# A transformer block on one core: the byte offsets of TensorE's two operands, two more column pairs by block products, four additions moved

## The chip, the cores and the metric

The kernel runs on one core of a Trainium2 chip. A core has five engines with queues of their own: TensorE (PE in the profile; its weight loads are listed as PEld), VectorE (DVE), ScalarE (ACT), GpSimd (POOL) and SyncE (SP, which here issues nearly all DMAs). The metric is the device time of one execution in microseconds (us). For the kernel before it is 1021.69 us, the median of three runs (1021.38 to 1025.06).

## The reference

One decoder block on x of 512 tokens by 1024 features, all in float32. Three sub-layers, each behind an RMSNorm whose result is scaled and shifted by vectors computed from c; a final RMSNorm ends it.

```python
u = modulate(rmsnorm(h, g_norm_ffn1[l]), sh1, sc1)
h = h + 0.5 * gt1 * swiglu(u, w_ffn1_in[l], w_ffn1_out[l])
u = modulate(rmsnorm(h, g_norm_mix[l]), sh2, sc2)
h = h + gt2 * token_mixing(u, cos, sin, w_in[l], ...)
u = modulate(rmsnorm(h, g_norm_ffn2[l]), sh3, sc3)
h = h + 0.5 * gt3 * swiglu(u, w_ffn2_in[l], w_ffn2_out[l])
...
def swiglu(u, w_in, w_out):
    a, b = jnp.split(u @ w_in, 2, axis=-1)
    return (jax.nn.silu(a) * b) @ w_out
```

The hidden width of `swiglu` is 2816, that is 22 tiles of 128. The token mixer is one wide projection of u, a pooling branch, dilated attention in three groups, two gates and an output projection. The change touches the two `swiglu` layers (FFN 1 and FFN 2 below) and where operands lie in memory; it does not change what is computed.

## The kernel before

Everything is kept transposed: features on the 128 partitions, tokens along the free dimension. h is eight tiles `H` of 128 x 512.

**Split operands.** TensorE runs its matmuls on float32r operands. For accuracy each operand is split into a rounded part and the rest: weights into `whi` and `wlo`, u into `UH` and `UL`, the hidden activations into `HI` and `HK`. A product is three matmuls, hi x hi, hi x lo and lo x hi (`mm3`, lines 321 to 325; `product`, lines 703 to 712, for the block products). In both the weights are the stationary operand, 128 x 128, and u or the hidden tile is the moving operand, of 512 or 256 columns.

**The weight stream.** Weights come in chunks of 128 x 1024 (some narrower), in the order of `self.order`, which `plan` (line 144) writes down for the whole kernel. A chunk is loaded to one of three `raw` buffers on SP's queue (`fetch`), rounded by ScalarE into the ring `whi` (`split_hi`, line 280) and the rest is written by VectorE into the ring `wlo` (`split_lo`, line 292). The rings hold `RING` columns; `room` (line 235) finds the place of the next chunk. `look` runs the split a few chunks ahead of the one that TensorE takes. In the built program `whi` starts at byte 13440 and `wlo` at byte 42112 of each partition, both 128 modulo 256, and every 128 x 128 tile of weights starts at that offset, since 128 columns are 512 bytes.

**Pairs and block products.** The input side of a FFN is worked in pairs j = 0 to 21: tile j of a and tile j of b. A plain pair (`ffn_pair`, line 653) is 2 x 8 x 3 = 48 matmuls of 512 columns. Two pairs together can be done by `duo` (line 714), which multiplies 2 x 2 blocks (features halved, tokens halved) with seven block products in place of eight, 7 x 24 = 168 matmuls of 256 columns. This asks for sums and differences of u's blocks (`u_steps`, line 664: four additions, then four splits into `S` tiles, named SH and SL in the profile) and for differences of weight chunks (`make`, line 222, on VectorE). u's four blocks lie in the tile `X`; two of these blocks, once added up, give the place for the weight differences (`self.X`), the two others become two more raw buffers. `PLAIN` says below which j pairs are plain: 8 in FFN 1, 4 in FFN 2.

**Order of FFN 1.** The row-by-row stage (`startup`, line 1385) goes through the eight tiles of u as they are normalised and fills all eight PSUM banks with the products of pairs 0 to 3 (lines 1481 to 1486, 192 matmuls of 512 columns). `ffn` (line 815) then works in the five `PARTS`: it computes pairs until two beyond those that the part needs, then the output stage of the part: eight output tiles of 128 x 512 over the part's hidden tiles. So part 0 has pairs 4 and 5 and its output stage, part 1 pairs 6 and 7, the block product of pairs 8 and 9, and its output stage, and so on. The output stages pop one entry of `self.todo` for each output tile; in part 0 these are the additions and splits of `u_steps`, in parts 2 and 3 the steps of the angles for the rotary embedding (`trig`). The last part ends in `out_tail` (line 482) with matmuls of 256 columns, whose first half of tokens feeds the next norm while the second half runs; `head` (line 600) of the next stage begins with matmuls of 256 columns for the same reason.

**Beside it.** The modulation vectors are computed by VectorE, one row of 128 x 1024 after another (`ada_do`, line 346, 1.2 us each, with a load of 512 KB on SP's queue). `bg` runs one. Rows 16 to 23 go beside pairs 4 and 5; rows 24 to 47 beside the tiles of pairs 6 and 7 (four) and the output stages of parts 1, 2 and 3 (eight, eight and four). FFN 2 has no such rows.

**Where u lies.** `UH` and `UL` are placed by `place_u` (line 455) at 0, 16 or 0 columns of a buffer that starts at 64 modulo 256 bytes, so at 64 for FFN 1 and FFN 2 and at 128 for the mixer. The hidden tiles, the mixer's tiles and `S0` start at 128, `S1` and `S2` at 64, after a filler `padb` of 48 columns (line 811).

Of the kernel before, what the change touches and what calls it, by code (L numbers as in the profile page):

```python
# [8 lines left out]
F32 = mybir.dt.float32  # L9
F32R = mybir.dt.float32r  # L10
# [100 lines left out]


FIRST = 4
RING = 7 * 1024


U_AT = (0, 16, 0)

PLAIN = {0: 8, 2: 4}
PARTS = ((0, 4), (4, 8), (8, 12), (12, 16), (16, 22))  # L120
NH = 6

# [14 lines left out]
class Kernel:  # L137
# [6 lines left out]
    def plan(self):  # L144
        (i1, o1), mix, (i2, o2) = chunk_widths()
        self.chunks = []
        for name, ws in (("wf1i", i1), ("wf1o", o1), ("wmix", mix), ("wf2i", i2), ("wf2o", o2)):
            off, rec = 0, []
            for w in ws:
                rec.append((name, off, w))  # L150
                off += P * w
            self.chunks.append(rec)
        f1i, f1o, mx, f2i, f2o = self.chunks


        self.loads, self.order, self.last = [], [], {}

        def plain(recs):
            for r in recs:
                n = len(self.loads)  # L160
                self.loads.append(r)
                self.last[n] = len(self.order)
                self.order.append((r[2], n, ("raw", n), None))

        def blocks(recs):
            n = len(self.loads)
            self.loads.extend(recs)
            r11, r12, r22, r21 = (("raw", n + i) for i in range(4))
            x0, x1 = ("x", 0), ("x", 1)
            for need, src, make in ((0, r11, None), (1, x0, (x0, r12, r11)), (2, x1, (x1, r22, x0)), (3, r21, None),  # L170
                                    (3, r12, (r12, r22, r12)), (3, r22, None), (3, x0, (x0, r21, x1))):
                for j, x in enumerate((r11, r12, r22, r21)):
                    if x == src or (make and x in make):
                        self.last[n + j] = len(self.order)
                self.order.append((D, n + need, src, make))

        def ffn(n, ins, outs, first):
            j, at = first, 0
            if first:
                plain(ins[:KT])  # L180
                at = KT
            for part, (k0, k1) in enumerate(PARTS):
                while j < pairs_before(n, part):
                    if j < PLAIN[n]:
                        plain(ins[at:at + 2])
                        j, at = j + 1, at + 2
                    else:
                        blocks(ins[at:at + 4])
                        j, at = j + 2, at + 4
                plain(outs[part * KT // 2:(part + 1) * KT // 2] if part + 1 < len(PARTS) else outs[-KT:])  # L190

        ffn(0, f1i, f1o, FIRST)
        base = len(self.order)
        plain(mx)
        ffn(2, f2i, f2o, 0)
        self.fetched = self.done = self.made = 0
        self.pos, self.held, self.retired, self.half = 0, None, [], None
# [37 lines left out]
    def room(self, i, held):  # L235


        w, u, at, pieces = self.order[i][0], self.unit(i), self.top, []
        for c in range(0, w, u):
            if at % RING + u > RING:  # L240
                at += RING - at % RING
            o = at % RING
            if pieces and pieces[-1][0] + pieces[-1][1].stop - pieces[-1][1].start == o:
                pieces[-1] = (pieces[-1][0], slice(pieces[-1][1].start, c + u))
            else:
                pieces.append((o, slice(c, c + u)))
# [10 lines left out]
    def split_hi(self):  # L257
# [2 lines left out]
        i = self.done  # L260
        if self.half or i == len(self.order):
            return False
        got = self.room(i, held)
        if got is None:
            assert i >= self.pos, "no room"
# [12 lines left out]
                    parts.append((slice(o + x.start - c.start, o + x.stop - c.start), x))  # L278
        for y, x in parts:
            self.nc.scalar.activation(self.hi[:, y], r[:, x], AF.Copy)  # L280
        if i + 1 < len(self.order) and self.order[i + 1][3] and self.order[i + 1][1] < self.fetched:
            self.make(i + 1)
        self.half = (r, parts)
        return True
# [170 lines left out]
    def place_u(self, n):  # L455
        self.UHv, self.ULv = (x[:, U_AT[n]:U_AT[n] + KT * T] for x in (self.UHall, self.ULall))
        self.UH, self.UL = ([x[:, k * T:(k + 1) * T] for k in range(KT)] for x in (self.UHv, self.ULv))

    def norm_steps(self, n, hs):

        t, done = {}, [0]
# [20 lines left out]
    def out_tail(self, ms, ksrc, gate, nxt, squares):  # L482
# [7 lines left out]
        for h, hs in enumerate((A, Bh)):  # L490
            for m in ms:
# [10 lines left out]
                for i, (hi, lo, uh, ul) in enumerate(ks):  # L502
                    if h == 1 and m == ms[1] and i == 3:
                        self.stats_t(self.B[6], A)
                    if h == 1 and m == ms[2] and i == 1:
                        self.spread(self.B[6], A)
                        self.place_u(nxt)
# [156 lines left out]
    def u_steps(self, n):  # L664
# [18 lines left out]
        def whole(u, k):  # L683
# [1 line left out]
            hi, lo = (y.rearrange("p (k t) -> p k t", k=KT)[:, x, :HT] for y in (self.UHv, self.ULv))  # L685
            return lambda: v.tensor_tensor(u.rearrange("p (k t) -> p k t", k=4), hi, lo, op=OP.add)

        last = split(3, a12)
        return ([whole(a11, 0), whole(a12, 4)] if n else []) + [add(a22, a21, a22, OP.add), split(0, a22), add(a21, a11, a21, OP.subtract), split(2, a21),
                add(a11, a22, a11, OP.subtract), split(1, a11), add(a12, a12, a11, OP.subtract)], last  # L690

    def step(self):

# [84 lines left out]
    def ffn2(self):  # L778
        self.put, self.now = [], 0
        bk = [self.nb() for _ in range(4)]  # L780
        self.head(2, bk, AF.Silu)
        self.todo, last = self.u_steps(2)
# [116 lines left out]
    def beside_out(self, part):  # L899

        if part == 0:
# [433 lines left out]
    def build(self):  # L1335
# [12 lines left out]
        self.UHall = tl("UH", KT * T + 16, F32R)  # L1348
        cst, self.eps = tl("cst", 163), tl("eps", 1)
        self.ULall = tl("UL", KT * T + 16, F32R)  # L1350
        self.place_u(0)
# [33 lines left out]
    def startup(self):  # L1385
# [166 lines left out]
```

## Time and profile before

| what | value |
|---|---|
| median of three runs | 1021.69 us (1021.38 to 1025.06) |
| the profiled execution, its own time | 1025.08 us |
| its span in the profile | 1023.3 us |
| granted TensorE clock | 0.998 of full speed |
| row-by-row stage of FFN 1 | 19.8 to 64.7 us |
| rest of FFN 1, with the tail | 64.7 to 366.4 us |
| mixer, from its head to its tail | 366.4 to 671.8 us |
| FFN 2, from its head | 671.8 to 1023.3 us |
| split of a 128 x 1024 chunk: ACT, then DVE | 1.05 us, 1.22 us |
| bytes from memory, mean rate | 135.8 MB, 135 GB/s |

The profile is one execution taken by the hardware profiler. An engine's busy time counts its instructions; the matmuls are pipelined, so the duration of one matmul in the timeline (0.28 us for 256 columns, 0.39 for 512) overlaps the next, and the price of a matmul is the distance from its start to the next one's. A stretch filled with equal matmuls and without waits gives this price as its length divided by their number. The three runs and the profiled execution differ by 3.7 us in all.

### The profile page before, as it was taken

Reading aid. Unit: us, or ns where it says so; the run is one execution under the profiler, and the core shown is the slowest. Engines: PE = TensorE matmul, PEld = TensorE weight load, DVE = VectorE, ACT = ScalarE, POOL = GpSimd, SP = SyncE. Lnnn points to the kernel's source line nnn. Section 1 sums busy time; section 2 is a strip of 40 time slices with the busy share of each in tenths; the row PEclk is TensorE's granted clock in tenths of the full one; section 3 lists DMA queues with packets and bytes.
Section 4 is the critical chain, followed back from the end, with each engine's and each line's share of the span. In section 5 each row is a group of like instructions: output and inputs, shape, how many; then the busy total and the mean of one; then the engine's idle time right before and its main releaser. Section 6 shows DMA issues by size and latency. Waiting matters only on the chain.

```text
span 1023.3 us, 15508 instructions
## 1 busy us (share of the span) xinstructions
PE 1012.1 (99%) x6364; PEld 914.9 (89%) x6364; DVE 753.2 (74%) x1082; ACT 434.8 (42%) x638; POOL 26.0 (3%) x30
## 2 busy tenths in 40 slices
PE   8999999999999999999999999999999999999997
PEld 7888898989999899889988888998899899998997
DVE  6969879889786777779446776577787776676754
ACT  5453352534445552334314333454365354352552
POOL 0000000000000000006100000000000000000001
PEclk9999999999999999999999999999999999999999
DMA  8856365555533513222154774322244234241312
GB/s 315 285 177 256 112 238 162 172 162 188 165 115 106 157 35 103 62 83 83 32 185 156 268 263 127 104 63 72 94 155 135 83 103 145 84 144 45 112 32 83
DMA packets 43113, 139.60 MB, mean 136 GB/s; under 512 B 4897, under 2 KB 8225, under 8 KB 43042
## 3 DMA queue, kind: packets, MB, share of 16 engines
q1 hardware_dynamic: 42354, 137.95, 41.3%
q8 instruction: 50, 0.82, 0.3%
q10 hardware_dynamic: 688, 0.66, 0.2%
q14 instruction: 21, 0.17, 0.1%
HBM read 135.82 MB, written 2.77 MB: 135 GB/s over the span
## 4 chain that ended last, share of the span: by engine, by line
PE 95%; DVE 3%; DMA 1%; ACT 0%; issue 0%; DVEq 0%; ACTq 0%
PE bank L323 17%; PE bank L324 17%; PE bank L325 17%; PE bank L710 10%; PE bank L712 10%; PE bank L711 10%; PE bank L1486 1%; PE bank L1484 1%; PE bank L1482 1%; PE bank L1080 1%; PE bank L1259 1%; PE bank L1411 1%; PE bank L1260 1%; PE bank L1261 1%; PE bank L1028 1%; PE bank L1057 1%
## 5 line engine op out<-in xcount | busy, mean ns | idle before, releaser
L292 DVE TENSOR_TENSOR wlo<-raw,whi 128x1024 fp32r<-128x1024 f32 (+2 forms) x151 | 175.5, 1165 | 69.0 <-ACT whi L280 68.8
L280 ACT ACTIVATE whi<-raw 128x1024 fp32r<-128x1024 f32 (+2 forms) x151 | 150.4, 1003 | 42.6 <-DVE raw L228 39.8
L323 PE MATMUL bank<-UH,whi 128*128 128x512 f32 (+1 forms) x432 | 159.0, 368 | 0.0
L324 PE MATMUL bank<-UL,whi 128*128 128x512 f32 (+1 forms) x432 | 154.9, 359 | 0.2 <-DVE UL L452 0.2
L325 PE MATMUL bank<-UH,wlo 128*128 128x512 f32 (+1 forms) x432 | 154.9, 359 | 0.0
L323 PE MATMUL bank<-HI,whi 128*128 128x512 f32 (+1 forms) x406 | 146.8, 362 | 0.0
L324 PE MATMUL bank<-HK,whi 128*128 128x512 f32 (+1 forms) x406 | 146.5, 361 | 0.0
L325 PE MATMUL bank<-HI,wlo 128*128 128x512 f32 (+1 forms) x406 | 146.5, 361 | 0.0
L710 PE MATMUL bank<-UH,whi 128*128 128x256 f32 x512 | 141.6, 277 | 0.0
L711 PE MATMUL bank<-UL,whi 128*128 128x256 f32 x512 | 141.6, 277 | 0.0
L712 PE MATMUL bank<-UH,wlo 128*128 128x256 f32 x512 | 141.6, 277 | 0.0
L292 DVE TENSOR_TENSOR wlo<-X,whi 128x1024 fp32r<-128x1024 f32 (+2 forms) x88 | 104.4, 1188 | 39.5 <-ACT whi L280 39.3
L710 PE MATMUL bank<-SH,whi 128*128 128x256 f32 x384 | 107.1, 279 | 0.3 <-ACT u L717 0.3
L711 PE MATMUL bank<-SL,whi 128*128 128x256 f32 x384 | 106.9, 278 | 0.0
L712 PE MATMUL bank<-SH,wlo 128*128 128x256 f32 x384 | 106.9, 278 | 0.0
L280 ACT ACTIVATE whi<-X 128x1024 fp32r<-128x1024 f32 (+2 forms) x88 | 89.3, 1028 | 33.1 <-DVE X L228 32.1
L711 PEld LDWEIGHTS bank<-UL,whi 128*128 128x128 f32 x512 | 96.1, 188 | 0.3
L710 PEld LDWEIGHTS bank<-UH,whi 128*128 128x128 f32 x512 | 96.1, 188 | 0.3
L712 PEld LDWEIGHTS bank<-UH,wlo 128*128 128x128 f32 x512 | 96.4, 188 | 0.0
L325 PEld LDWEIGHTS bank<-UH,wlo 128*128 128x128 f32 x432 | 81.3, 188 | 12.8
L324 PEld LDWEIGHTS bank<-UL,whi 128*128 128x128 f32 x432 | 81.5, 189 | 12.3 <-issue 0.5
L323 PEld LDWEIGHTS bank<-UH,whi 128*128 128x128 f32 x432 | 81.4, 189 | 11.9 <-issue 0.5
(225 smaller groups left out, 1748.5 us busy)
## 6 DMA issues: line engine op xcount, KB each, us to landing
ada<-wada SPq DMA_DIRECT2D x47, 512.0 KB, 5.0
raw<-wmix SPq DMA_DIRECT2D x44, 512.0 KB, 3.9
raw<-wf1i SPq DMA_DIRECT2D x34, 512.0 KB, 4.5
raw<-wf2i SPq DMA_DIRECT2D x30, 512.0 KB, 3.6
X<-wf2i SPq DMA_DIRECT2D x14, 512.0 KB, 3.5
cs<-wada SPq DMA_DIRECT2D x12, 512.0 KB, 3.5
AR<-wada SPq DMA_DIRECT2D x12, 512.0 KB, 3.9
raw<-wf2o SPq DMA_DIRECT2D x12, 512.0 KB, 3.6
```

The costliest lines, as they stand in the source:

```text
L280: self.nc.scalar.activation(self.hi[:, y], r[:, x], AF.Copy)
L292: self.nc.vector.tensor_tensor(self.lo[:, y], r[:, x], self.hi[:, y], op=OP.subtract)
L323: M(ps, hi, uh, start=start, stop=False)
L324: M(ps, hi, ul, start=False, stop=False)
L325: M(ps, lo, uh, start=False, stop=stop)
L710: M(o, hi, uh, start=start and p == 0 and k == 0, stop=False, skip_group_check=True)
L711: M(o, hi, ul, start=False, stop=False, skip_group_check=True)
L712: M(o, lo, uh, start=False, stop=k == 3, skip_group_check=True)
L1028: M(S[:, o + i * P:o + i * P + P], qz[:, (2 * i + h) * P:(2 * i + h + 1) * P], k[:, toks], start=True, stop=True)
L1057: nc.tensor.transpose(b[:, i * P:i * P + P], p[:, i * P:i * P + P], self.ident)
L1080: M(o, pt[:, blk * P:blk * P + P], v, start=i == 0, stop=i == len(srcs) - 1)
L1259: M(b, self.UH[k][:, c::4], hi, start=k == 0, stop=False)
```

## The change

Four parts.

- u is placed at 128 modulo 256 bytes for all three sub-layers, by fillers of 16 columns; `place_u` goes. A chunk in the set `shifted` starts 16 columns (64 bytes, `SHIFT`) further in the ring, at 192 modulo 256 bytes. Shifted are all block products' chunks, the first four chunks of the mixer and of FFN 2 (their heads), the last three of FFN 1, the last two of the mixer and the last four of FFN 2 (their tails). The ring has 128 columns more. `S0` moves to 192, `S1` and `S2` to 128.
- `PLAIN[0]` goes from 8 to 6: pairs 6 and 7 of FFN 1 are done by a block product.
- `u_steps` returns additions and splits apart. For FFN 1 the four additions run at the end of the row-by-row stage, ahead of the silu of pairs 0 to 3; the splits are popped in part 0's output stage. FFN 2 runs them in the same order as before.
- A flag `ready` keeps weight differences from being made until these splits are issued, since they are written over u's blocks.

```diff
-RING = 7 * 1024
-U_AT = (0, 16, 0)
-PLAIN = {0: 8, 2: 4}
+RING = 7 * 1024 + 128
+SHIFT = 16
+PLAIN = {0: 6, 2: 4}
...
         def blocks(recs):
             n = len(self.loads)
+            self.shifted.update(range(len(self.order), len(self.order) + 7))
...
+        def shift(i):
+            self.shifted.update(range(len(self.order) - i, len(self.order)))
...
                     if j < PLAIN[n]:
                         plain(ins[at:at + 2])
+                        if n and j < 2:
+                            shift(2)
...
         ffn(0, f1i, f1o, FIRST)
+        shift(3)
         base = len(self.order)
         plain(mx)
+        self.shifted.update(range(base, base + 4))
+        shift(2)
         ffn(2, f2i, f2o, 0)
+        shift(4)
...
     def room(self, i, held):
+        shift = SHIFT if i in self.shifted else 0
+        at += (shift - at) % 64
         for c in range(0, w, u):
             if at % RING + u > RING:
-                at += RING - at % RING
+                at += RING - at % RING + shift
...
     def split_hi(self):
+        if self.order[i][3] and not self.ready:
+            return False
...
     def u_steps(self, n):
-        last = split(3, a12)
-        return ([whole(a11, 0), whole(a12, 4)] if n else []) + [add(a22, a21, a22, OP.add), split(0, a22), add(a21, a11, a21, OP.subtract), split(2, a21),
-                add(a11, a22, a11, OP.subtract), split(1, a11), add(a12, a12, a11, OP.subtract)], last
+        adds = [add(a22, a21, a22, OP.add), add(a21, a11, a21, OP.subtract), add(a11, a22, a11, OP.subtract),
+                add(a12, a12, a11, OP.subtract)]
+        return ([whole(a11, 0), whole(a12, 4)] if n else []) + adds, [split(2, a21), split(1, a11), split(0, a22), split(3, a12)]
...
     def open_sums(self):
         for i in range(3):
+            if i < 2:
+                bp.tile([P, (SHIFT, 64 - SHIFT)[i]], F32, name=f"padb{i}")
             self.S.append([bp.tile([P, 4 * HT], F32R, name=f"S{x}{i}") for x in "HL"])
-            if i == 0:
-                bp.tile([P, 48], F32, name="padb")
...
     def beside_out(self, part):
-            self.todo, last = self.u_steps(0)
+            self.todo, last = self.splits[:3], self.splits[3]
+            self.ready = False
+            self.todo.append(lambda: setattr(self, "ready", True))
...
     def startup(self):
         self.bg_fetch()
+        adds, self.splits = self.u_steps(0)
+        for f in adds:
+            f()
         for j in range(FIRST):
```

More of the change, by code (lines that the diff above doesn't have):

```diff
@@ L156, in plan @@
         self.loads, self.order, self.last = [], [], {}
+        self.shifted = set()
         def plain(recs):
@@ L192, in plan @@
         ffn(0, f1i, f1o, FIRST)
+        shift(3)
         base = len(self.order)
         plain(mx)
+        self.shifted.update(range(base, base + 4))
+        shift(2)
         ffn(2, f2i, f2o, 0)
+        shift(4)
         self.fetched = self.done = self.made = 0
+        self.ready = True
         self.pos, self.held, self.retired, self.half = 0, None, [], None
@@ L280, in split_hi @@
             self.nc.scalar.activation(self.hi[:, y], r[:, x], AF.Copy)
-        if i + 1 < len(self.order) and self.order[i + 1][3] and self.order[i + 1][1] < self.fetched:
+        if i + 1 < len(self.order) and self.order[i + 1][3] and self.ready and self.order[i + 1][1] < self.fetched:
             self.make(i + 1)
@@ L453, in norm_b @@
                                             op0=OP.add, op1=OP.subtract)
-    def place_u(self, n):
-        self.UHv, self.ULv = (x[:, U_AT[n]:U_AT[n] + KT * T] for x in (self.UHall, self.ULall))
-        self.UH, self.UL = ([x[:, k * T:(k + 1) * T] for k in range(KT)] for x in (self.UHv, self.ULv))
     def norm_steps(self, n, hs):
@@ L506, in out_tail @@
                         self.spread(self.B[6], A)
-                        self.place_u(nxt)
                         step = self.norm_steps(nxt, A)
@@ L781, in ffn2 @@
         self.head(2, bk, AF.Silu)
-        self.todo, last = self.u_steps(2)
+        adds, (s2, s1, s0, last) = self.u_steps(2)
+        self.todo = adds[:3] + [s0, adds[3], s2, adds[4], s1, adds[5]]
         do = lambda n: [self.todo.pop(0)() for _ in range(n)]
@@ L1347, in build @@
         self.H = [tl(f"H{k}", T) for k in range(KT)]
-        self.UHall = tl("UH", KT * T + 16, F32R)
+        tl("pad0", 16)
+        self.UHv = tl("UH", KT * T, F32R)
         cst, self.eps = tl("cst", 163), tl("eps", 1)
-        self.ULall = tl("UL", KT * T + 16, F32R)
-        self.place_u(0)
+        tl("pad1", 16)
+        self.ULv = tl("UL", KT * T, F32R)
+        self.UH, self.UL = ([x[:, k * T:(k + 1) * T] for k in range(KT)] for x in (self.UHv, self.ULv))
         self.AR = tl("AR", 2 * T)
```

## The prediction

> **What bounds the kernel now.** I read three views: the page for the busiest engine and the chain, the busy times by stretch for the price of each stage, and the timeline of one stretch for the spacing of matmuls. "PE" is TensorE, "DVE" VectorE, "ACT" ScalarE.
>
> ```profile
> PE 1012.1 (99%) x6364; PEld 914.9 (89%) x6364; DVE 753.2 (74%) x1082; ACT 434.8 (42%) x638; POOL 26.0 (3%) x30
> PE 95%; DVE 3%; DMA 1%; ACT 0%; issue 0%; DVEq 0%; ACTq 0%
> ```
>
> The span is a stream of matmuls, and 95% of the chain that ended last is PE. A busy PE can still hide waits, so the stretches are next. Columns: stretch, its length, then busy time and instructions of PE, weight loads, DVE, ACT and GpSimd, then clock and DMA.
>
> ```profile
> 64.70:87.10 22.40, 22.40 (x98) 18.05 (x97) 18.00 (x25) 11.19 (x16) 0.00 (x0) 1.00 0.59 208
> 87.10:108.90 21.80, 21.80 (x98) 18.04 (x97) 19.85 (x26) 6.77 (x8) 0.00 (x0) 1.00 0.52 181
> 108.90:131.30 22.40, 22.40 (x98) 17.95 (x97) 16.93 (x21) 6.46 (x8) 0.00 (x0) 1.00 0.45 137
> 131.30:150.50 19.20, 19.20 (x170) 19.20 (x169) 15.72 (x16) 12.19 (x15) 0.00 (x0) 1.00 0.66 232
> ...
> 373.00:390.30 17.30, 17.30 (x147) 17.30 (x146) 11.10 (x21) 6.82 (x11) 0.00 (x0) 1.00 0.30 92
> 678.80:695.20 16.40, 16.40 (x147) 16.40 (x146) 10.40 (x20) 10.53 (x21) 0.00 (x0) 1.00 0.24 70
> ```
>
> In order: FFN 1's pairs 4 and 5, its first output stage, pairs 6 and 7 (each 96 matmuls of 512 columns; the counts include neighbours cut by the border), the block products of pairs 8 and 9 (168 of 256 columns), and 144 matmuls of 256 columns of the mixer's head and of FFN 2's head. The clock is 1.00 in all. Equal work differs: 22.40 against 21.80 us is 233.3 against 227.1 ns for one matmul of 512; 17.30 against 16.40 is 120.1 against 113.9 ns for one of 256. What differs is where the moving operand starts. The weights (whi, wlo) start at 128 modulo 256 bytes throughout. u of FFN 1 and 2 starts at 64, all other moving operands, u of the mixer too, at 128. Call an operand in step with the weights when both start at the same place modulo 128, out of step when they are 64 apart. So: 512 columns, in step 227, out of step 233; 256 columns, in step 120, out of step 114. The timeline has the second pair inside one block product, starts in the first column:
>
> ```profile
> 131.27 0.28 PE L710 MATMUL bank<-UH,whi 128*128 128x256 f32 x1
> ...
> 134.00 0.28 PE L710 MATMUL bank<-SH,whi 128*128 128x256 f32 x1
> ...
> 136.86 0.29 PE L710 MATMUL bank<-SH,whi 128*128 128x256 f32 x1
> ```
>
> 24 matmuls on u (64) take 2.73 us, 113.8 ns each; the next 24, on S0 (which starts at 128), 2.86 us, 119.2 ns. Nothing waits in either.
>
> **The change part by part.** After it u starts at 128 everywhere. Weights start at 192 (SHIFT) in all work of 256 columns, except the tails' first tile (m = 4 of FFN 1, m = 3 of FFN 2, m = 5 of the mixer) and the rows of v, and stay at 128 for 512 columns. S0 moves to 192, S1 and S2 to 128.
>
> 1. Row-by-row stage, 192 matmuls of 512 columns, 19.8 to 64.7 us: out of step to in step. 44.9 x 21.80/22.40 = 43.7: -1.2 us. DVE sets each row's inputs every 5.32 us (line 452's starts 46.07 and 51.39), PE then needs 5.45 a row, so PE stays the bound.
> 2. Pairs 4, 5, and FFN 2's pairs 2, 3 (22.40 us from 695.2): -0.6 each, -1.2 us.
> 3. Pairs 6 and 7 become one block product: 22.4 less 19.2: -3.2 us.
> 4. The 16 block products that stay, and FFN 2's head: out of step before and after, S0 in step before and after: 0, if the difference of the two starts is what counts. No row has weights at 192, so the bounds are 114 and 120 ns; I take 114, the row with the same difference.
> 5. Tails and the mixer's head: 108 + 192 + 96 + 144 = 540 matmuls of 256 columns go from in to out of step: 540 x 6.2 ns = -3.3 us, with the same bounds (0 to -3.3).
> 6. FFN 2's head waits for its norm today (the eleventh matmul comes 0.37 us late, on UL of line 452). 39 matmuls between that norm's statistics and the head get 6.2 ns shorter: +0.2 us. The mixer's head has 1.6 us of slack there (UL[1] ready at 365.96, used at 367.62).
> 7. The four additions on u's blocks move from the first output stage to the end of the row-by-row stage, four DVE instructions of 1.21 us, 4.6 us, and no DMA. There DVE stands idle:
>
> ```profile
> 58.01 1.23 DVE L292 TENSOR_TENSOR wlo<-raw,whi 128x1024 fp32r<-128x1024 f32 x1 [0.56 <-ACT whi L280]
> 63.89 0.69 DVE L635 TENSOR_TENSOR hf<-sl,bank 128x512 f32<-128x512 f32 x1 [4.65 <-ACT sl L642]
> ```
>
> They end at 63.8, where the first silu product now begins. With PE 1.2 us ahead that product is about 1 us late; behind it stands the split of pair 4's second tile (done 67.45, needed near 69), which keeps over 1 us: 0. Without that cover the cost is at most 4.6.
> 8. The new block product asks DVE for about 15.1 us (FFN 2's three: 45.34 in 57.7 us) where pairs 6 and 7 took 16.93; in the first output stage four additions go (-4.8) and two weight differences come (+2.4). The flag `ready` holds those back until the fourth of its eight tiles, some 11 us ahead of use: 0. Pairs 6 and 7 no longer run four of the 24 modulation rows (1.2 us on DVE each, and a 512 KB load on SP's queue); these fall to the output stage of part 3. It then has eight, as part 2's has, whose DVE runs late until 243.7; there PE stops once:
>
> ```profile
> 243.60 0.28 PE L712 MATMUL bank<-UH,wlo 128*128 128x256 f32 x1
> 244.18 0.39 PE L710 MATMUL bank<-SH,whi 128*128 128x256 f32 x1 [0.31 <-ACT u L717]
> ```
>
> 244.18 less 243.60 is 0.58, where 0.11 is usual: 0.5 us. I charge the same for part 3: +0.5 (bounds 0, as part 1's stage, and twice it).
> 9. A ring of 7296 columns cuts 30 chunks in two, and three more chunks are split: 30 more instructions each on ACT and DVE, whose fixed part is 0.15 us (1024 columns 1.22, 512 0.69). 4.5 us spread over the span under PE: 0.
>
> Sum: -1.2 - 1.2 - 3.2 - 3.3 + 0.2 + 0.5 = -8.2 us. The profiled execution took 1025.1 us round a span of 1023.3; it would take 1016.9 round 1015.1. It lies 3.4 above the median of the runs, 1021.7, which goes to **1013.5**.
>
> **The rivals.**
>
> *The position of the moving operand alone counts* (slower). If PE is quick at 256 columns because u starts at 64, the weights' shift does nothing. Then 16 x 144 block matmuls and 192 of FFN 2's head go from 113.8 to 119.5: 2496 x 5.7 = +14.2; S0 at 192 gains 16 x 24 x 5.7 = -2.2; the new product costs 144 x 119.5 + 24 x 113.8 = 19.9 against 22.4: -2.5; steps 1 and 2 stay, -2.4; step 5 is 0; with +0.5: +7.6, **1029.3**. It decides from some 2.3 ns for each of the 2496, where it eats the other terms. For it: every weight in the trace starts at 128, so no row tells difference from position. Against it: a position that costs the moving stream something should cost it at both lengths, yet 64 is dearer at 512 (+6) and cheaper at 256 (-6). That fits two streams that meet differently. The Trainium skill ("TensorE: Matmul & The Clock Gate", the section "Step-by-step: what each phase is for") has a rule on this rival's side: the moving operand and the weight load have a read port each, so that loading the next weights takes nothing from the running matmul. By that rule the weights' place can't matter, which is 1029.3; the rows of 114 and 120 ns under one and the same weights neither need nor refute it.
>
> *Step 5 gives nothing*, since DVE and ACT pace the tails' and heads' short steps: 1013.5 + 3.3 less the 0.2 of step 6 = **1016.6**. For it: FFN 2's head does wait at 114 ns. Against: the rest of that head runs 144 matmuls at 113.9.
>
> *DVE becomes the bound of FFN 1*: two block products back to back after pairs 4 and 5, then three loaded output stages. If each stage stops PE as part 2's does and the first product starts a product late (2.7 us): 2 x 0.5 + 2.7 more, **1017.2**. Against: FFN 2 runs three back to back at 19.2 each.
>
> **How the numbers follow.** Forecast 0.65, position alone 0.18, step 5 nothing 0.09, DVE 0.08. A measurement of this kernel tells about 0.5% (5.1 us) from no change. Faster by more (under 1016.6): 0.65 and half of the two middle cases, 0.73; the rest of these within it, with a half-true position rival, 0.11; slower 0.16. The forecast's own range is 1011.5 to 1016; taking in both middle cases and spread between runs, 1011 to 1019.5; the position rival is left out.
>
> **What would show it.** Rows: pairs 4 and 5 in 21.8 us; 24 block matmuls on u with weights at 192 in 2.73 (right) or 2.87 (the position rival); S0's still 2.86; the mixer's 144 in 16.4; 19.2 us where pairs 6 and 7 stood; a stop under 1 us in the block products after part 3's output stage. Any wait of PE on DVE at 63 to 70 us would undo step 7. An unchanged 120 ns in the tails with 114 in the block products would undo step 5 alone.

## The result, and the profile after

The changed kernel takes 1016.92 us (median of nine runs, 1016.21 to 1020.15). The kernel before, run beside it, takes 1022.52 (nine runs, 1021.38 to 1025.06). The ratio is 0.9951, with a 95% interval of 0.9938 to 0.9964: faster by about half a per cent. A second series gave 1017.23 against 1023.0, ratio 0.9945 (0.9928 to 0.9963).

The profiled execution of the changed kernel took 1020.15 us round a span of 1018.4, against 1025.08 round 1023.3: 4.9 us less in both, where the prediction's sum was 8.2 less.

One plain source of spread first. The first matmul of the row-by-row stage starts at 19.8 us in both these profiles, at 16.6 in another profile of the changed kernel, and between 16.3 and 17.8 in those of its edits below. What differs is TensorE's own pace in the opening: the small matmuls ahead of the stage start every 213 ns in both profiles here, and every 112 ns from 11.4 us on in the other one. The two profiled executions of the changed kernel took 1020.15 and 1016.66 us, and 3.2 of these 3.5 us lie ahead of that matmul; so it is likely, though only these two have a trace, that this makes the two clumps in its runs, near 1016.5 and near 1019.9. Single executions are therefore compared below *from that first matmul to the end*: 1003.5 us before, 998.5 after, and 998.3 in the other execution of the changed kernel.

The page of the changed kernel, first the busy times, then the chain that ended last:

```profile
PE 1006.6 (99%) x6436; PEld 914.9 (90%) x6436; DVE 764.5 (75%) x1119; ACT 442.2 (43%) x674; POOL 26.2 (3%) x30
PE 90%; DVE 7%; ACT 1%; issue 1%; DMA 1%; SPq 0%; DVEq 0%; ACTq 0%
```

72 more matmuls (168 of 256 columns in place of 96 of 512) in 5.5 us less. DVE has 11 us more to do, and its share of the chain has gone from 3% to 7%: somewhere the matmuls now end up behind it. The stretches say where. Columns as before: stretch, length, busy time and instructions of PE, weight loads, DVE, ACT, GpSimd, then clock, DMA share, GB/s.

```profile
63.50:85.20 21.70, 21.70 (x97) 17.98 (x96) 17.17 (x24) 10.57 (x17) 0.00 (x0) 1.00 0.54 183
107.00:145.50 38.50, 38.50 (x337) 38.50 (x336) 33.36 (x36) 23.11 (x30) 0.00 (x0) 1.00 0.49 159
227.60:267.00 39.40, 39.23 (x337) 39.02 (x336) 34.65 (x43) 21.15 (x28) 0.00 (x0) 1.00 0.56 182
288.80:328.40 39.60, 39.29 (x338) 39.08 (x337) 32.39 (x38) 20.36 (x28) 0.00 (x0) 1.00 0.45 140
369.00:385.40 16.40, 16.40 (x147) 16.40 (x146) 9.83 (x20) 6.20 (x11) 0.00 (x0) 1.00 0.20 65
690.30:712.80 22.50, 22.00 (x98) 17.90 (x97) 17.94 (x19) 10.18 (x14) 0.00 (x0) 1.00 0.20 65
712.80:734.90 22.10, 22.10 (x98) 17.96 (x98) 17.38 (x20) 7.96 (x10) 0.00 (x0) 1.00 0.31 100
```

In order: pairs 4 and 5 (21.7 us, 22.4 before); the block products of pairs 6 to 9 (38.5, where 22.4 + 19.2 stood); two block products after part 2's output stage (39.4) and two after part 3's (39.6; 38.5 before); the mixer head's 144 matmuls (16.4, 17.3 before); FFN 2's pairs 2 and 3 (22.5, no better than before); and its first output stage (22.1, where 21.8 is usual). Three stretches, the two of 39.4 and 39.6 us and the one of 22.5, have PE busy for less than their length: there it stood still.

Measured from the start of one stage's first matmul to the next one's, and set against the prediction's steps (us):

| step | forecast | before | after | measured |
|---|---|---|---|---|
| 1 row-by-row stage | -1.2 | 44.88 | 43.65 | -1.2 |
| 2 pairs 4 and 5 | -0.6 | 22.40 | 21.76 | -0.6 |
| 2 FFN 2's pairs 2 and 3 | -0.6 | 22.40 | 22.58 | +0.2 |
| 3 pairs 6 to 9 | -3.2 | 41.61 | 38.53 | -3.1 |
| 4 other block products, where nothing stops | 0 | 38.52 for two | 38.53 | 0 |
| 5 tails and mixer's head | -3.3 | 109.53 | 107.47 | -2.1 |
| 6 FFN 2's head | +0.2 | 23.43 | 23.55 | +0.1 |
| 7 four additions moved | 0 | | | 0 |
| 8 block products after part 3 | +0.5 | 38.52 | 39.55 | +1.0 |
| 8 and those after part 2 | 0 | 39.11 | 39.41 | +0.3 |
| 9 ring: FFN 2's first output stage | 0 | 21.78 | 22.04 | +0.3 |
| from the first matmul to the end | -8.2 | 1003.46 | 998.55 | -4.9 |

(Step 5's stages are FFN 1's tail 34.5 to 34.1, the mixer's head 23.9 to 22.9, its tail 18.1 to 17.9 and the end of the kernel 33.0 to 32.5; 0.2 us of small losses lie outside the rows.) So 3.3 us are missing: 1.0 in FFN 2 behind its head, 1.2 in the tails and the mixer's head, and 0.8 in the block products after parts 2 and 3. The rest agrees to 0.3 us. In the other execution of the changed kernel the total is the same within 0.3 us, but not its parts: the mixer's head takes 23.5 us there, and the block products after parts 2 and 3 take 38.86 and 39.16.

**The moved additions.** The timeline of VectorE at the end of the row-by-row stage of the changed kernel; start, duration, and in brackets the idle time ahead:

```profile
59.15 5.00 DVE L683 TENSOR_TENSOR X<-X 128x1024 f32<-128x1024 f32 x4
64.06 0.68 DVE L648 TENSOR_TENSOR hf<-sl,bank 128x512 f32<-128x512 f32 x1
```

The four additions fill what was an idle gap of 4.65 us, and the silu product starts at 64.06 (63.89 before). TensorE waits for none of it.

**The rhythm of 256 columns.** TensorE's timeline at the first block product of pairs 6 and 7, one line where each block product begins (24 matmuls from one to the next):

```profile
106.98 0.28 PE L723 MATMUL bank<-UH,whi 128*128 128x256 f32 x1
...
109.81 0.28 PE L723 MATMUL bank<-SH,whi 128*128 128x256 f32 x1
...
112.69 0.28 PE L723 MATMUL bank<-SH,whi 128*128 128x256 f32 x1
...
115.43 0.28 PE L723 MATMUL bank<-UH,whi 128*128 128x256 f32 x1
```

The first 24 are out of step and take 2.83 us, 118 ns each; the next 24, on S0, are in step and take 2.88, 120 ns each; the third 24, on S1, again out of step, take 2.74, 114 ns each. So "out of step" comes in two rhythms, 118 and 113. Both were in the trace of the kernel before. Where a block product came behind an output stage, as at part 1's, its first 24 matmuls on u took 2.83 us there too:

```profile
172.26 0.28 PE L710 MATMUL bank<-UH,whi 128*128 128x256 f32 x1
...
175.09 0.28 PE L710 MATMUL bank<-SH,whi 128*128 128x256 f32 x1
```

The prediction's row of 2.73 us is the one block product that came behind matmuls of 512 columns out of step. The same two rhythms appear in FFN 1's tail of the changed kernel, three matmuls from line to line:

```profile
348.97 0.28 PE L341 MATMUL bank<-HI,whi 128*128 128x256 f32 x1
...
349.32 0.28 PE L341 MATMUL bank<-HI,whi 128*128 128x256 f32 x1
...
359.77 0.28 PE L341 MATMUL bank<-HI,whi 128*128 128x256 f32 x1
...
360.11 0.28 PE L341 MATMUL bank<-HI,whi 128*128 128x256 f32 x1
```

0.35 us for three ahead of the norm's statistics (118 ns each; with the in-step tile, 120, all 99 take 11.73 us), and 0.34 (113 each) behind the float32 matmuls that spread the norm's factor over the partitions. Before the change the 99 took 11.87, at 120.

**The stops.** TensorE once after part 3's output stage, then once in FFN 2's pair 2:

```profile
299.86 0.28 PE L725 MATMUL bank<-UH,wlo 128*128 128x256 f32 x1
300.45 0.39 PE L723 MATMUL bank<-SH,whi 128*128 128x256 f32 x1 [0.31 <-ACT u L730]
...
701.40 0.39 PE L342 MATMUL bank<-UL,whi 128*128 128x512 f32 x1
702.28 0.50 PE L343 MATMUL bank<-UH,wlo 128*128 128x512 f32 x1 [0.50 <-DVE wlo L310]
```

The first is 590 ns from start to start, as part 2's had been. The second is 880 ns where 227 is usual, and waits for VectorE's half of a weight split. That split is late because its chunk came late. ScalarE's splits during FFN 2's head and pair 2, in the changed kernel, then in the kernel before:

```profile
676.26 1.05 ACT L298 ACTIVATE whi<-raw 128x1024 fp32r<-128x1024 f32 x1
683.00 1.04 ACT L298 ACTIVATE whi<-raw 128x1024 fp32r<-128x1024 f32 x1
698.61 1.99 ACT L298 ACTIVATE whi<-raw 128x1024 fp32r<-128x1024 f32 x2
```

```profile
681.23 1.04 ACT L280 ACTIVATE whi<-raw 128x1024 fp32r<-128x1024 f32 x1
687.97 1.04 ACT L280 ACTIVATE whi<-raw 128x1024 fp32r<-128x1024 f32 x1
691.51 1.05 ACT L280 ACTIVATE whi<-raw 128x1024 fp32r<-128x1024 f32 x1
```

Before, three chunks are split by 692.6. After, only two, and the third comes at 698.6 together with a fourth, just when VectorE also makes the sums of u's blocks. The reason is room in the ring: FFN 2's head has shifted chunks, its pairs 2 and 3 have not, and the step from 192 back to 128 costs 48 columns; a chunk cut at the ring's end may use up to 128 more. Seven chunks with both are 7168 + 48 + 128 = 7344 columns, and the ring has 7296; worked through by the rule of `room`, this is what seven chunks take from FFN 2's first, second or third one on. That this is the cause is put to the test below.

### The profile page after: what moved, and what is told of

It is laid out like the page before. It is cut to its first block, busy times and chain, and to the rows that moved or that the text cites. A ratio compares the mean times of both kernels' runs of the same rounds, so it can differ in the third digit from the quotient of the medians.

```text
span 1018.4 us, 15737 instructions
## 1 busy us (share of the span) xinstructions
PE 1006.6 (99%) x6436; PEld 914.9 (90%) x6436; DVE 764.5 (75%) x1119; ACT 442.2 (43%) x674; POOL 26.2 (3%) x30
## 4 chain that ended last, share of the span: by engine, by line
PE 90%; DVE 7%; ACT 1%; issue 1%; DMA 1%; SPq 0%; DVEq 0%; ACTq 0%
PE bank L341 16%; PE bank L342 16%; PE bank L343 16%; PE bank L723 10%; PE bank L725 10%; PE bank L724 10%; PE bank L1501 1%; PE bank L1505 1%; PE bank L1503 1%; PE bank L1097 1%; DVE wlo L310 1%; PE bank L1276 1%; DVE AR L364 1%; PE bank L1430 1%; DVE cs L364 1%; DVE H L868 1%
## 5 line engine op out<-in xcount | busy, mean ns | idle before, releaser
L310 DVE TENSOR_TENSOR wlo<-raw,whi 128x1024 fp32r<-128x1024 f32 (+6 forms) x166 | 174.4, 1061 | 67.6 <-ACT whi L298 67.0
L298 ACT ACTIVATE whi<-raw 128x1024 fp32r<-128x1024 f32 (+6 forms) x166 | 149.7, 919 | 45.7 <-DVE raw L242 42.0
L310 DVE TENSOR_TENSOR wlo<-X,whi 128x1024 fp32r<-128x1024 f32 (+4 forms) x106 | 111.7, 1063 | 33.1 <-ACT whi L298 32.8
L298 ACT ACTIVATE whi<-X 128x1024 fp32r<-128x1024 f32 (+4 forms) x106 | 95.7, 927 | 46.1 <-DVE X L242 45.3
L724 PEld LDWEIGHTS bank<-UL,whi 128*128 128x128 f32 x544 | 102.3, 188 | 0.3
L723 PEld LDWEIGHTS bank<-UH,whi 128*128 128x128 f32 x544 | 102.1, 188 | 0.3
L725 PEld LDWEIGHTS bank<-UH,wlo 128*128 128x128 f32 x544 | 102.3, 188 | 0.0
L342 PEld LDWEIGHTS bank<-HK,whi 128*128 128x128 f32 x406 | 76.3, 188 | 11.8 <-DVE HK L651 0.4
L341 PEld LDWEIGHTS bank<-HI,whi 128*128 128x128 f32 x406 | 76.5, 188 | 11.5
L343 PEld LDWEIGHTS bank<-HI,wlo 128*128 128x128 f32 x406 | 76.3, 188 | 11.6
```

The costliest lines, as they stand in the source:

```text
L310: self.nc.vector.tensor_tensor(self.lo[:, y], r[:, x], self.hi[:, y], op=OP.subtract)
L341: M(ps, hi, uh, start=start, stop=False)
L342: M(ps, hi, ul, start=False, stop=False)
L343: M(ps, lo, uh, start=False, stop=stop)
L723: M(o, hi, uh, start=start and p == 0 and k == 0, stop=False, skip_group_check=True)
L724: M(o, hi, ul, start=False, stop=False, skip_group_check=True)
```

## The experiments

Each starts from the changed kernel; the two theories of the first one are the prediction's forecast (A: what counts is the difference between the places of the two operands) and its position rival (B).

**1. All weights at 128.** Chunks are no longer shifted, and S0 goes to 128 as well, so that everything in the block products and tails is in step.

```diff
-        shift = SHIFT if i in self.shifted else 0
+        shift = 0
...
-                bp.tile([P, (SHIFT, 64 - SHIFT)[i]], F32, name=f"padb{i}")
+                bp.tile([P, 64], F32, name=f"padb{i}")
```

> The changed kernel with every weight left at 128 modulo 256 bytes, and S0, S1 and S2 at 128 like u, so that all operands are in step. Theory A, the difference of the two starts sets the spacing: all matmuls of 256 columns take 120 ns, a block product of two pairs 20.16 us where it takes 19.26, 17 x 0.9 = +15.3 us, the two heads and the tails +2.5, less up to 1.5 of stops on VectorE that the slower stream covers: span 1034 to 1036. Theory B, the start of the moving operand alone sets it, and u at 128 is quick: nothing moves in the block products, S1 and S2 unchanged too, span 1018 to 1020.

1032.26 us; from the first matmul 1013.4, 14.9 more than the changed kernel. The two block products of pairs 6 to 9:

```profile
104.30:144.60 40.30, 40.30 (x338) 40.30 (x336) 34.46 (x36) 22.93 (x30) 0.00 (x0) 1.00 0.48 159
```

40.30 us for 336 matmuls is 120 ns each, without a wait. For the matmuls on u, S1 and S2 nothing but the place of the weights differs from the changed kernel, where the quick ones take 113. So A holds and the position rival falls. The span, 1030.5 us, is 3.5 under A's band; 2.7 of this is that the execution reached its first matmul earlier than the profile of the changed kernel did. FFN 2's pairs 2 and 3 take 21.79 us here and nothing stops: with no shifted chunks there is no step back, and no room lost.

**2. Pairs 6 and 7 plain again.**

```diff
-PLAIN = {0: 6, 2: 4}
+PLAIN = {0: 8, 2: 4}
```

> The changed kernel with pairs 6 and 7 plain again (their four modulation rows beside them again, too); offsets and everything else as changed. Counted from the first matmul of the row-by-row stage, since the time until then varies between executions (16.3 to 19.8 us so far): the changed kernel takes 998.6 us from there. Theory: pairs 6 and 7 plain and in step 21.8 us, so 41.1 for pairs 6 to 9 where the changed kernel takes 38.5, +2.6; the block products after part 3's output stage fall from 39.55 to 38.5, -1.0; total 1000.2. Rival, the stop after part 3 isn't these rows: 1001.2.

1016.65 us; from the first matmul 998.3, as the changed kernel. Pairs 6 to 9, then the block products after part 3's output stage, then FFN 2's pairs 2 and 3:

```profile
103.70:144.80 41.10, 41.10 (x265) 37.32 (x264) 29.93 (x36) 17.24 (x23) 0.00 (x0) 1.00 0.54 184
...
287.60:326.10 38.50, 38.50 (x338) 38.50 (x337) 27.80 (x29) 19.38 (x27) 0.00 (x0) 1.00 0.34 113
...
687.80:709.60 21.80, 21.80 (x99) 18.03 (x98) 17.14 (x18) 9.57 (x13) 0.00 (x0) 1.00 0.21 67
```

The pairs cost 2.55 us more than with the block product (41.08 against 38.53), and what had stopped runs free or nearly so: -1.02 after part 3, -0.55 after part 2 (38.86 against 39.41, with a stop of 0.2 us left), -0.79 in FFN 2's pairs and -0.25 in its output stage, together -2.61. So between these two executions what the new block product gains is paid back in full by what stops later. The four modulation rows go back to pairs 6 and 7 here, which fits part 3 running free (experiment 3 tests it). FFN 2 has the same shifts as in the changed kernel but comes to another place of the ring, since the order ahead of it has other shifted chunks: by the rule of `room`, seven chunks from any of FFN 2's first five on take 7280 columns here, which fit in 7296. That this frees it is worked out, not tried alone. Part 2's figure moves between executions of one kernel (experiment 4).

**3. Four modulation rows beside the new block product.** They run behind its block products 1, 2, 4 and 5, and no longer in part 3's output stage.

```diff
             self.product(bank, u, start)
+            if j == FIRST + 2 and i in (1, 2, 4, 5):
+                self.bg()
```

> The four modulation rows that pairs 6 and 7 used to run go beside products 1, 2, 4 and 5 of the first block product; everything else as changed. Theory A, they overload VectorE in part 3's output stage: the two block products after it go from 39.55 us back to 38.5 to 38.7, the span falls by 0.9 to 1.0 us, to 1017.4. Rival, the stop comes from the angles' steps or from the cut chunks: it stays, 39.4 to 39.6, span 1018.4. Second risk: the first block product takes 15.1 + 4.6 us of VectorE in 19.3 and stops TensorE by up to 0.4 us there.

1016.82 us; from the first matmul 997.3, 1.2 less than the changed kernel. The block products of pairs 6 to 9, then those after part 3:

```profile
104.90:143.80 38.90, 38.90 (x338) 38.87 (x336) 38.09 (x44) 22.81 (x30) 0.00 (x0) 1.00 0.62 210
...
286.50:325.10 38.60, 38.60 (x338) 38.56 (x338) 27.96 (x30) 19.54 (x28) 0.00 (x0) 1.00 0.36 114
```

The stop after part 3 is gone: 38.52 against 39.55. In both executions of the changed kernel and in experiments 4 to 7, all with eight rows there, these block products took 38.8 to 39.6 us; with four (here and in experiments 2 and 9) they took 38.5. So step 8's mechanism is right, with one thing added: part 1's output stage has eight rows too, and no profile shows a stop in what follows it. Parts 2 and 3 have the steps of the angles beside the rows, so it seems to take the two together.

The block products of pairs 6 to 9 take 0.34 us more here, but that the rows cost this isn't shown. Experiment 5 has no rows there and took as long (38.86). In both executions one matmul there came late, by less than 0.1 us, and the 47 behind it ran at 118 ns in place of 113, up to the next product on S0.

**4. A ring of 128 columns more.**

```diff
-RING = 7 * 1024 + 128
+RING = 7 * 1024 + 256
```

> The changed kernel with a ring of 7424 columns in place of 7296. Theory A, in FFN 2's head the step from shifted to unshifted chunks and the wrap leave no room for a seventh chunk, so the third split there is made late, on top of the block sums: with room, FFN 2's pairs 2 and 3 take 21.8 us (22.5 now) and the output stage after them 21.8 (22.1 now), span 1017.4. Rival, the 30 cut chunks load VectorE: the cuts stay about as many, so both stretches stay within 0.2 us, span 1018.4.

1014.6 us; from the first matmul 996.1, 2.4 less than the changed kernel. FFN 2's pairs 2 and 3 and its first output stage:

```profile
685.80:707.50 21.70, 21.70 (x98) 17.98 (x97) 17.03 (x18) 9.49 (x13) 0.00 (x0) 1.00 0.21 67
707.50:729.30 21.80, 21.80 (x97) 18.01 (x97) 17.21 (x20) 7.71 (x9) 0.00 (x0) 1.00 0.31 98
```

21.79 and 21.80 us instead of 22.58 and 22.04. The third split is back within the head. So it was the ring's room. Of the other 1.4 us of the gain, 1.2 come from the block products after parts 2 and 3 (38.83 and 38.90). Those two differ between executions of one kernel (the changed kernel had 39.41 and 39.55, another time 38.86 and 39.16), so it isn't shown that the ring gave them.

**5. One more tile out of step ahead of the tails.** The rhythm of a tail might depend on where in the stream the first out-of-step matmul comes, so the shifted chunks begin two chunks earlier: the tails' first tile of 256 columns and the last tile of 512 are out of step too.

```diff
-        shift(3)
+        shift(5)
...
-        shift(2)
+        shift(4)
...
-        shift(4)
+        shift(6)
```

> The three tails shifted from two tiles earlier: the first tile of 256 columns and the last tile of 512 columns before it are out of step too. Theory A, the 118 ns of the tails is a rhythm taken over from the 512-column stream in step before them, and an out-of-step lead gives 114: FFN 1's tail 0.6 us shorter, the mixer's 0.5, FFN 2's 0.6, less 60 matmuls of 512 columns at +6.5 ns (0.4): span 1017.1. Rival, 118 belongs to these operands whatever came before: only the first tiles gain 2 ns for each of 108 (0.2), and the lead costs 0.4: span 1018.6.

1016.69 us; from the first matmul 998.6, no gain. In FFN 1's tail, six matmuls from line to line:

```profile
341.95 0.28 PE L341 MATMUL bank<-HI,whi 128*128 128x256 f32 x1
...
342.66 0.28 PE L341 MATMUL bank<-HI,whi 128*128 128x256 f32 x1
```

Still 118 ns each (99 matmuls in 11.66 us, 11.73 without this edit), and the tile of 512 columns now costs 0.12 to 0.16 us more. The idea fell: one more tile out of step in front does not bring the quick rhythm.

**6. The additions back in part 0's output stage.** In the old order, an addition ahead of each split. The flag `ready` then comes with the eighth tile instead of the fourth.

```diff
-            self.todo, last = self.splits[:3], self.splits[3]
+            a, (s2, s1, s0, last) = self.adds, self.splits
+            self.todo = [a[0], s0, a[1], s2, a[2], s1, a[3]]
...
-        for f in adds:
-            f()
+        self.adds = adds
```

> The changed kernel with the four additions back in part 0's output stage, each ahead of its split as before; the flag is then set by the eighth tile, not the fourth. Theory A, the move is needed: the first weight difference is made only when the first block product already runs, and TensorE stops for 1 to 3 us in the first block products (39.5 to 41.5 us for the pair of them, 38.53 now). Rival, VectorE's work was hidden there as well: 38.5 to 38.7, and the row-by-row stage and pairs 4 and 5 stay at 43.7 and 21.8.

1021.63 us; from the first matmul 1002.7, 4.2 more than the changed kernel. TensorE where the first block product passes to its second:

```profile
106.98 0.28 PE L725 MATMUL bank<-UH,wlo 128*128 128x256 f32 x1
109.64 0.38 PE L723 MATMUL bank<-SH,whi 128*128 128x256 f32 x1 [2.37 <-ACT whi L298]
```

From one start to the next 2.65 us pass, where 0.12 is usual, until ScalarE has split a weight difference; two more such gaps, of 1.08 and 1.46 us, follow in the next product. The two block products take 43.65 us instead of 38.53: +5.1, more than was expected of either theory. The longest wait is for a weight difference, and `ready` lets these begin only with the eighth tile here. So against the old order the move is needed for the new block product: without it, pairs 6 to 9 cost 2.0 us more than before the change (41.61). Another order with an earlier flag was not tried.

**7. A break in FFN 1's tail.** Four small float32 matmuls into an unused bank, ahead of the tile m = 5. They add work and change no output.

```diff
                 ks = tiles[m]
+                if nxt == 1 and h == 0 and m == ms[1]:
+                    for t in range(0, T, P):
+                        nc.tensor.matmul(self.B[7][:, t:t + P], self.ones, self.ident, start=True, stop=True)
```

> The changed kernel with four float32 matmuls of 128 columns into an unused bank ahead of the second tile (m = 5) of FFN 1's tail, like those that spread a norm later in the tail. Theory A, any such break brings the out-of-step stream into the quick rhythm: the 54 matmuls after it take 113.4 ns, not 117.7 (-0.2 us), for 0.45 us of its own. Rival, the rhythm belongs to these operands: 117.7 stays.

1017.56 us; from the first matmul 998.2. The tail behind them, six matmuls from line to line:

```profile
344.93 0.28 PE L341 MATMUL bank<-HI,whi 128*128 128x256 f32 x1
...
345.61 0.28 PE L341 MATMUL bank<-HI,whi 128*128 128x256 f32 x1
```

0.68 us for six, 113.3 ns each, where the unbroken tail ran at 118. So the slow rhythm belongs to the stream's history, not to the tail's tiles, their places or their work beside other engines. The break costs more than it gains: FFN 1's tail takes 34.81 us in place of 34.14. The total is no longer only because the block products after parts 2 and 3 lost 1.0 us less in this execution.

**8. S0 out of step too.** The weights stay at 192, S0 goes from 192 to 128.

```diff
-                bp.tile([P, (SHIFT, 64 - SHIFT)[i]], F32, name=f"padb{i}")
+                bp.tile([P, 64], F32, name=f"padb{i}")
```

> The changed kernel with S0 at 128 like S1 and S2, so that all seven block products are out of step. Theory A, out-of-step matmuls have two rhythms, 113.4 and 117.7 ns, the stream enters a block product in the slow one after the 512 columns in step, and the product on S0, in step, brings it into the quick one: without it all 336 matmuls of two block products take 117.7, 39.5 us where 38.53 are taken now. Rival, the operands alone decide: S0's 24 matmuls go from 120 to 114, 38.2 us for the two.

1024.04 us; from the first matmul 1004.7, 6.2 *more* than the changed kernel. The block products of pairs 6 to 9:

```profile
104.70:144.30 39.60, 39.60 (x338) 39.60 (x337) 33.77 (x36) 23.15 (x30) 0.00 (x0) 1.00 0.48 159
```

39.57 us, 117.8 ns for each matmul, the whole time. The 24 matmuls on S0 that looked like a loss (120 ns, the only ones in step) are what carries the other 120 into the quick rhythm. With them out of step, all 168 stay in the slow one. Where TensorE stops for a moment in this kernel, the products run faster (38.71 and 39.00 for two): a stop can break the slow rhythm too. It can also break the quick one: behind the stop after part 3 in the changed kernel's profile, 72 matmuls on u ran at 117.8 that took 113.3 in the kernel before and in the changed kernel's other execution.

**9. Ring and rows together, and the changed kernel again.** The ring of experiment 4, and the rows spread out: two beside each of the block products in FFN 1 until they run out, and in the output stages of parts 1 to 3 only one for each two tiles.

```diff
-RING = 7 * 1024 + 128
+RING = 7 * 1024 + 256
...
+            if self.ada_free is not None and self.ada_stop == 48 and i in (2, 5):
+                self.bg()
...
-                        if n == 0 and part:
+                        if n == 0 and part and i == 0:
```

> The changed kernel with the ring of 7424 columns, and the 24 modulation rows of parts 1 to 3 spread out: two beside each of the six block products there (products 2 and 5) and four, not eight, beside each output stage. If the stops in the block products after parts 2 and 3 and in FFN 2's pairs 2 and 3 are VectorE's load and the ring's room, all go: 38.5 to 38.6 us for each two block products of FFN 1, 21.8 for FFN 2's pairs and for the output stage after them, 995.5 us from the first matmul of the row-by-row stage (998.5 as changed), and 3.0 us less than the changed kernel in the runs: about 1013.9 where that is 1016.9. Rival, rows beside the block products stop TensorE there, as four in the first one did by 0.34: 996 to 997 from the start.

> The changed kernel once more, on the chip of the version that should be the best: 1016 to 1017.5 us; 998.5 us from the first matmul of the row-by-row stage, with stops of 0.2 to 0.6 us after parts 2 and 3 that vary, and the same 22.6 us in FFN 2's pairs 2 and 3.

1014.4 us (five runs, 1013.92 to 1014.98), ratio to the kernel before 0.9913 (0.9896 to 0.9931); the unedited changed kernel beside it 1017.23 (six runs, 1016.17 to 1019.23), the one already given above. From the first matmul 995.1 against 998.3: 3.2 us less. The block products of pairs 6 to 9, those after parts 2 and 3, and FFN 2's pairs 2 and 3:

```profile
104.60:143.10 38.50, 38.50 (x337) 38.48 (x336) 37.10 (x42) 22.84 (x30) 0.00 (x0) 1.00 0.56 188
...
225.20:263.80 38.60, 38.60 (x338) 38.56 (x338) 33.15 (x42) 20.09 (x27) 0.00 (x0) 1.00 0.55 180
285.60:324.10 38.50, 38.50 (x338) 38.50 (x337) 27.91 (x31) 19.18 (x27) 0.00 (x0) 1.00 0.36 115
...
685.60:707.40 21.80, 21.80 (x99) 18.04 (x98) 17.13 (x18) 9.56 (x13) 0.00 (x0) 1.00 0.21 68
```

All four stretches are at their free price. This version beats both kernels: 8.6 us under the kernel before by the medians, of which the change as it stands brings 5.8.

## Why the prediction was right, and where it was not

It forecast 1013.5 us, with 1011.0 to 1019.5 as the range, and faster by over half a per cent as likeliest. 1016.9 lies in the range, though outside the forecast's own (1011.5 to 1016), and the measured gain, 0.5%, is just what can be told from no change. The medians of nine runs each differ by 5.6 us, where the sum was 8.2.

**Right, by its own steps.** Steps 1, 3 and 6 came out as worked out, within 0.15 us, and step 2 did in FFN 1. Step 4 chose the row with the same difference of starts (114 ns) rather than the same position (120), and the block products' 38.53 us and experiment 1's 40.3 bear the choice out. The sign it named, 2.73 us for 24 matmuls on u, holds except for the first 24 behind an output stage, which take 2.83. Part of this is luck: the choice gave no reason to keep S0 in step, and counted it as the dear part of a block product, while experiment 8 shows that the 113 ns of the others hang on it. The position rival's 1029.3 is refuted, and so here, as the prediction used it, is the rule on its side (the Trainium skill, "TensorE: Matmul & The Clock Gate", section "Step-by-step: what each phase is for": loading the next weights takes nothing from the running matmul): moving the weights alone by 64 bytes took the spacing from 113 to 120 ns. Step 7's cover was there, and the additions cost nothing; experiment 6 shows what the step did not price, that leaving them where they were, in the old order, would have cost 5.1 us in the block products of pairs 6 to 9.

**Mis-sized: step 5, -2.1 in place of -3.3.** It took 114 ns from block products and FFN 2's head for all 540 matmuls. The mixer's head reached that in this profile (its 144 went from 17.35 to 16.42 us), and in the other execution it didn't (17.04). Most of the tails' matmuls run at 118. The step assumed one price for "out of step"; there are two, which depend on what ran just before, and the rows for 118 were in the trace of before, in the first block product behind each output stage. The rival "step 5 gives nothing" has nearly the measured time (1016.6), but not the mechanism: the term gave 2.1 us, half of it in the tails, and what is missing besides lies in steps 2, 8 and 9.

**Mis-sized in this profile: step 8, +1.3 in place of +0.5.** The mechanism was right, as experiment 3 shows: a stop of 0.6 us from start to start after part 3's output stage, 0.5 more than usual. The rest is rhythm: behind the stop the block products fell into the slow one, which the term had no price for, and part 2's two lost 0.3 the same way. In the other execution the stop is as long (0.62), the quick rhythm returns behind it, and the two stages together come to +0.4, as forecast. The rival "DVE becomes the bound" named this, with a first product late by 2.7 us that did not come.

**Failed: step 9, "0", and with it step 2's FFN 2 half.** The step counted the instructions that the new ring adds, but not the room that it leaves. The step back from 192 to 128 and the cut at the end of the ring keep one chunk fewer ahead in FFN 2's head. Pairs 2 and 3 came to +0.2 instead of -0.6, and the output stage behind them to +0.3. Experiment 4 gives both back with 128 columns, as experiment 1 does without shifted chunks.

## What to carry to other kernels

When a stream of matmuls is the bound, lay out the relative start of the moving operand and of the weights, and measure the spacing separately for each length and for what came just before: the difference between 113, 118 and 120 ns was worth more here (14.9 us in experiment 1, 6.2 in experiment 8) than the new block product (3.1), and a piece that looked like the slow one (S0, in step) was the one that made the rest quick. When an edit changes the layout of a prefetch ring, count how many chunks still fit at the worst step and wrap, not only the instructions that it adds. When work is taken off the critical engine, look for the stage whose margin falls below nothing; here a new block product's 2.6 us was paid back by a few short stops, and 128 columns of ring with the small background rows spread out recovered it.

## What the runs showed of the hardware that had not been expected

- Two rhythms for the same matmuls. Matmuls of 256 columns whose moving operand and weights start 64 bytes apart follow each other either every 113.3 ns or every 117.8 ns, each steadily for as long as nothing breaks it (experiment 8: all 336 of a stage at 117.8). Behind matmuls of 512 columns in step it was the slow one in every profile; behind S0's 24 matmuls in step it was the quick one. In step there is one, 120. For 512 columns it is 227 in step and 233 out of step, the other way round.
- What decides the rhythm at the entry is open. Matmuls in step ahead are not enough: behind the 18 of a tail's first tile it was the slow one, in experiment 7 even where the quick one ran ahead of them. One more tile out of step in front changes nothing (experiment 5). Small float32 matmuls between don't settle it either: the quick one followed experiment 7's, but the mixer head's 144, with the same small matmuls ahead of them both times, took 16.42 us in one execution of the changed kernel and 17.04 in another.
- A short hitch can cost several times its length: one matmul less than 0.1 us late left the stream in the slow rhythm, and 0.3 us were lost (pairs 6 to 9 in experiments 3 and 5).
- The opening ran at two paces. Its small matmuls started every 213 ns, and from some time on every 112; when that came moved the first matmul of the row-by-row stage from 16.6 to 19.8 us in two executions of the changed kernel, which is more than most edits here are worth. The granted clock reads 1.00 in both stretches.
